# Rotating queries and keys before their norm factor in a two-layer diffusion transformer block

## The chip, the cores and the metric

One core of one Trainium2 chip runs the whole kernel as a single program. The metric is the device time of one execution in microseconds; smaller is better.

## The reference

Two layers work on 1024 image tokens and 256 context tokens of width 1024. Layer 0 mixes a windowed attention (8 query heads, 2 key heads) with a differential attention (4 heads, each with a pair of queries and keys); layer 1 is a gated linear attention, which the change does not touch. In layer 0 each query and key head of 64 numbers is normalised, and for image tokens rotated by its row and column in the token grid:

```python
def rms_norm(x, g):
    xf = x.astype(jnp.float32)
    y = xf * lax.rsqrt(jnp.mean(xf * xf, axis=-1, keepdims=True) + EPS)
    return (y * g.astype(jnp.float32)).astype(x.dtype)

def rope_1d(x, pos):
    ...
    return jnp.concatenate([x1 * cos - x2 * sin, x2 * cos + x1 * sin], axis=-1)

def project(h):
    ...
    qa = rms_norm(qa.reshape(Bn, T, A_HEADS, HEAD_DIM), a_qn)
    ka = rms_norm(ka.reshape(Bn, T, A_KV_HEADS, HEAD_DIM), a_kn)
    ...
qa_x = rope_axial(qa_x, rows, cols)
ka_x = rope_axial(ka_x, rows, cols)
```

The norm factor is one number per token and head, the gain one per place in the head.

## The kernel before

Layer 0's projections and attention are cut into six units, each with its share of the heads: units 0 and 1 belong to the windowed attention (`famA`, 4 query heads and 1 key head), units 2 to 5 to the differential attention (2 and 2). Unit 0 is projected first, beside the loading and the modulation of the inputs. Then, for u = 1 to 6, `layer0_heads` weaves the attention of unit u - 1 with the projection of unit u (for u = 6 with the gates). The windowed attention thus runs beside the projections of units 1 and 2, and the differential one beside those of 3 to 5. The order of each engine's instructions is set when the kernel is built, from the program order, priorities and a model of the times; on the chip every engine works its queue in that order.

A unit has ten token tiles of 128: eight of image tokens, and tiles 8 and 9 of context tokens, which are not rotated. For each, `l0_proj` multiplies (L399) into a PSUM tile `proj` of 384 columns (query heads, key heads, values), and `l0_qkv` (L749) turns it into queries and keys. `l0_qkv` in order:

- In units 0 to 2, where `proj` has four or two banks, it reads PSUM directly (`raw = ps`). In units 3 to 5, with one bank, ACT first copies the tile to SBUF (L163, a `qs` tile).
- ACT squares it into a `qs` tile (L766), DVE sums per head (L768) and scales and adds the epsilon (L769), and POOL raises to the power -0.5 (L223).
- The values are split into a high and a low part (L163, L774).
- DVE multiplies by the norm factor (L776).
- For image tokens the product is multiplied by the cosine table (L784, two instructions, on DVE in units 0 to 2, on POOL in 3 to 5) and, with the halves of each head exchanged, by the sine table (L787, four instructions on POOL), and both are added (L789, on DVE or POOL likewise). Context tokens are multiplied by the gain instead (L793, DVE).
- The result is split into `hb` (L163 and L412, or L807 and L811 on POOL), which TensorE transposes (L817, L821).

The `qs` tiles come from a ring of three (`QS = 3`), which the output gates (L694, L696) use as well in units 0 to 3. `rope_tables` (L500) multiplies the cosine and sine tables by the gains for queries and keys; it runs once for units 0 and 1 and once for units 2 to 5, and its products (L509) are on POOL. Raw weights of the beginning, the modulation weights (L268) and the first two units' projection weights (L584), are staged in a ring of `AW = 17` tiles `aw` of 128x512; SP issues all these loads in order. In the windowed attention POOL also scales the probabilities (L897) and forms the low parts of their transposes (L913).

Of the kernel before, what the change touches and what calls it, by code (L numbers as in the profile page):

```python
# [15 lines left out]
ALU = mybir.AluOpType  # L16
# [3 lines left out]
P = 128  # L20
# [19 lines left out]
AW = 17  # L40
# [93 lines left out]
class K:  # L134
# [307 lines left out]
    def layer0_heads(self, es, esw):  # L442
# [4 lines left out]
        self.pp = self.pool(es, "l0p")  # L447
        with ExitStack() as es1:
            ap = self.ap = self.pool(es1, "l0a")
            self.psum(T="017", O="2", proj="3456")  # L450
            self.condition(ap)
            self.xn = {}
            self.l0_x(4)
            self.staged = 0
            self.hspare = self.st(self.lp, [P, 2, NT * P], "k", F32R, bufs=2).rearrange("p a c -> p (a c)")[
                :, 0:2048].rearrange("p (t a k c) -> p t a k c", t=2, a=2, k=4)
            st = self.l0_state(0)
            drain(self.l0_proj(0, st, True))
# [41 lines left out]
    def rope_tables(self, fam):  # L500

        nc = self.nc
        self.tabs = []
        for j in range(2):
            raw = self.st(self.ap, [P, 512], "sc", bufs=2).rearrange("p (t d) -> p t d", t=NX)
            nc.sync.dma_start(raw, self.a["rope"][:, j])
            t = self.st(self.pp, [P, NX, 2, 64], f"tab{j}")
            for q in range(2):
                nc.gpsimd.tensor_tensor(t[:, :, q, :], raw,  # L509
                                        self.gain[:, 2 * q + j, :].unsqueeze(1).to_broadcast([P, NX, 64]),  # L510
                                        op=ALU.mult)
# [237 lines left out]
    def l0_qkv(self, famA, i, ps, st):  # L749
# [13 lines left out]
        else:  # L763
            raw = ps
        sq = qs()
        nc.scalar.activation(sq[:, 0:nh, :].rearrange("p a d -> p (a d)"), raw[:, 0:w], AF.Square)  # L766
        ss = self.st(pp, [P, 8], "qss", bufs=2)
        nc.vector.tensor_reduce(ss[:, 0:nh], sq[:, 0:nh, :], axis=AX.X, op=ALU.add)  # L768
        nc.vector.tensor_scalar(ss[:, 0:nh], ss[:, 0:nh], 1.0 / 64, EPS, op0=ALU.mult, op1=ALU.add)  # L769
# [5 lines left out]
        xn = qs()  # L775
        (nc.vector if raw is ps else self.by("xn")).tensor_tensor(xn[:, 0:nh, :], raw[:, 0:w].rearrange("p (h d) -> p h d", d=64),  # L776
                                r[:, 0:nh].unsqueeze(2).to_broadcast([P, nh, 64]), op=ALU.mult)
        rq = qs()
        groups = [(0, nq, 0), (nq, nk, 1)]
        if i < NX:  # L780
            m = qs()
            for h0, n, q in groups:
                cosv = self.tabs[0][:, i, q, :].unsqueeze(1).to_broadcast([P, n, 64])
                self.by("cos").tensor_tensor(rq[:, h0:h0 + n, :], xn[:, h0:h0 + n, :], cosv, op=ALU.mult)  # L784
                for s in range(2):
                    sv = self.tabs[1][:, i, q, 32 * s:32 * s + 32].unsqueeze(1).to_broadcast([P, n, 32])
                    nc.gpsimd.tensor_tensor(m[:, h0:h0 + n, 32 * s:32 * s + 32],  # L787
                                            xn[:, h0:h0 + n, 32 - 32 * s:64 - 32 * s], sv, op=ALU.mult)
            self.by("rot").tensor_tensor(rq[:, 0:nh, :], rq[:, 0:nh, :], m[:, 0:nh, :], op=ALU.add)  # L789
        else:  # L790
            for h0, n, q in groups:
                gv = self.gain[:, 2 * q, :].unsqueeze(1).to_broadcast([P, n, 64])
                nc.vector.tensor_tensor(rq[:, h0:h0 + n, :], xn[:, h0:h0 + n, :], gv, op=ALU.mult)  # L793
        hb = self.st(pp, [P, 6, P], "hb", F32R, bufs=1)
        flat = hb.rearrange("p a d -> p (a d)")
        if famA:

            self.split(hb[:, 0:4, 0:64], hb[:, 0:4, 64:128], rq[:, 0:4, :], ("hb", "hblo"))
            kk = rq[:, 4:5, :].to_broadcast([P, 2, 64])
            self.split(hb[:, 4, :].rearrange("p (a d) -> p a d", a=2), hb[:, 5, :].rearrange("p (a d) -> p a d", a=2), kk, ("hb", "hblo"))  # L800
            nqb = 4
        else:
# [917 lines left out]
```

## Time and profile before

| | us |
|---|---|
| median of 3 runs | 1592.39 |
| lowest, highest | 1588.01, 1595.9 |
| the profiled execution | 1597.08 |
| its span | 1595.3 |

| engine | busy us | share of the span |
|---|---|---|
| TensorE, matmul | 1482.9 | 93% |
| TensorE, weight load | 1302.5 | 82% |
| DVE | 1017.0 | 64% |
| ACT | 792.4 | 50% |
| POOL | 579.6 | 36% |

A line such as L787 is line 787 of the kernel. Names before the arrow are what an instruction writes, those behind it what it reads. "PE" is TensorE's matmul, "PEld" its weight load, "SPq" the queue of SyncE that issues DMAs. The idle time before an instruction is put down to whoever released it last.

### The profile page before, as it was taken

Reading aid. Unit: us, or ns where it says so; the run is one execution under the profiler, and the core shown is the slowest. Engines: PE = TensorE matmul, PEld = TensorE weight load, DVE = VectorE, ACT = ScalarE, POOL = GpSimd, SP = SyncE. Lnnn points to the kernel's source line nnn. Section 1 sums busy time; section 2 is a strip of 40 time slices with the busy share of each in tenths; the row PEclk is TensorE's granted clock in tenths of the full one; section 3 lists DMA queues with packets and bytes.
Section 4 is the critical chain, followed back from the end, with each engine's and each line's share of the span. In section 5 each row is a group of like instructions: output and inputs, shape, how many; then the busy total and the mean of one; then the engine's idle time right before and its main releaser. Section 6 shows DMA issues by size and latency. Waiting matters only on the chain.

```text
span 1595.3 us, 26832 instructions
## 1 busy us (share of the span) xinstructions
PE 1482.9 (93%) x9460; PEld 1302.5 (82%) x9460; DVE 1017.0 (64%) x2488; ACT 792.4 (50%) x2153; POOL 579.6 (36%) x857
## 2 busy tenths in 40 slices
PE   6897998999899999999999899989989999997998
PEld 4897977888798877688898777878878998896897
DVE  3787678768667666577765767638854536237565
ACT  3665667776756655466645634345642413224111
POOL 1756777988745554247100000001111212112111
PEclk9898999999999999999999999999999999999999
DMA  9732314322231565623323368655673635425542
GB/s 343 301 145 91 120 67 126 126 70 97 83 115 68 175 230 185 199 83 116 104 80 129 123 198 295 249 187 188 231 242 108 237 132 194 166 94 182 168 149 106
DMA packets 108399, 251.30 MB, mean 158 GB/s; under 512 B 10372, under 2 KB 58500, under 8 KB 94440
## 3 DMA queue, kind: packets, MB, share of 16 engines
q1 hardware_dynamic: 108264, 249.58, 46.1%
q8 instruction: 75, 1.23, 0.3%
q14 instruction: 60, 0.49, 0.1%
HBM read 196.78 MB, written 52.76 MB: 156 GB/s over the span
## 4 chain that ended last, share of the span: by engine, by line
PE 65%; DVE 8%; DMA 7%; ACT 4%; issue 3%; POOL 2%; SPq 0%; ACTq 0%; DVEq 0%; POOLq 0%
PE proj L399 40%; PE SX L1021 4%; PE T L1034 2%; PE AD L242 2%; PE S L399 1%; PE O L942 1%; DMA wraw<-in_w_out 1%; DMA wraw<-in_w_head 1%; PE T L931 1%; PE O L1048 1%; PE O L1046 1%; PE O L1047 1%; PE T L1462 1%; ACT p L993 1%; DMA h<-g_d 1%
## 5 line engine op out<-in xcount | busy, mean ns | idle before, releaser
L399 PE MATMUL proj<-w,h 128*128 128x384 f32 (+2 forms) x2544 | 555.2, 359 | 9.1 <-DVE qs L696 3.8
L399 PEld LDWEIGHTS proj<-w,h 128*128 128x128 f32 x2544 | 437.1, 192 | 49.8 <-DVE qs L696 5.4
L399 PE MATMUL proj<-h,w 128*128 128x256 f32 x1800 | 268.3, 291 | 14.0 <-DVE w L412 2.9
L399 PEld LDWEIGHTS proj<-h,w 128*128 128x128 f32 x1800 | 241.3, 194 | 27.4 <-DVE w L412 4.5
L993 ACT ACTIVATE p<-SX,bnm 128x512 f32<-128x512 f32 (+1 forms) x208 | 124.3, 610 | 52.2 <-DVE bnm L986 38.0
L1444 POOL TENSOR_SCALAR Ts<-U,alpha 128x256 f32<-128x256 f32 x64 | 36.9, 577 | 244.4 <-DVE U L1440 244.4
L913 POOL TENSOR_TENSOR wt<-praw,wt 128x512 fp32r<-128x512 f32 (+1 forms) x96 | 114.8, 1209 | 25.5 <-ACT wt L912 20.6
L1021 PE MATMUL SX<-k,q 128*128 128x512 f32 (+1 forms) x416 | 109.0, 371 | 3.4 <-ACT p L993 3.3
L981 DVE TENSOR_REDUCE bnm<-SX 128x1 f32<-128x512 f32 x128 | 86.2, 685 | 39.9 <-PE SX L1021 39.2
L223 POOL TENSOR_TENSOR qr<-qss,mhalf 128x4 f32<-128x4 f32 (+1 forms) x60 | 65.6, 1094 | 67.5 <-DVE qss L769 62.7
L1021 PEld LDWEIGHTS SX<-k,q 128*128 128x128 f32 x416 | 69.0, 190 | 19.8 <-ACT p L993 7.1
L1440 DVE SCALAR_TENSOR_TENSOR U<-U,alpha,S 128x256 f32<-128x256 f32 x64 | 30.6, 478 | 81.4 <-PE S L399 65.1
L787 POOL TENSOR_TENSOR qs<-qs,tab 128x64 f32<-128x64 f32 (+1 forms) x192 | 73.0, 406 | 11.2 <-DVE qs L776 3.3
L223 POOL TENSOR_TENSOR brr<-brs,mhalf 128x2 f32<-128x2 f32 x20 | 16.6, 831 | 164.3 <-DVE brs L1067 145.2
L414 ACT CAST wt<-T 128x512 fp32r<-128x512 f32 (+1 forms) x104 | 50.8, 511 | 43.9 <-PE T L1034 43.6
L415 DVE TENSOR_TENSOR wt<-T,wt 128x512 fp32r<-128x512 f32 (+1 forms) x104 | 59.1, 580 | 13.6 <-ACT wt L414 13.2
L911 ACT COPY praw<-T 128x512 f32<-128x512 f32 (+1 forms) x96 | 49.6, 542 | 34.8 <-PE T L931 34.2
L414 ACT CAST kmt<-T 128x128 fp32r<-128x128 f32 x72 | 18.7, 266 | 95.0 <-PE S L399 48.2
L897 POOL TENSOR_SCALAR p<-p,arz 128x640 f32<-128x640 f32 (+2 forms) x80 | 59.7, 759 | 15.9 <-DVE arz L895 10.4
L223 POOL TENSOR_TENSOR nr<-nms,mhalf 128x1 f32<-128x1 f32 x20 | 11.7, 586 | 146.4 <-DVE nms L339 146.4
L399 PE MATMUL proj<-w,ohl 128*128 128x512 f32 x240 | 62.0, 402 | 2.6 <-DVE ohl L741 1.7
L414 ACT CAST w<-wraw 128x768 fp32r<-128x768 f32 (+2 forms) x48 | 33.7, 727 | 59.9 <-DMA wraw<-in_w_head 37.1
(310 smaller groups left out, 3395.4 us busy)
## 6 DMA issues: line engine op xcount, KB each, us to landing
h<-hT_d SPq DMA_DIRECT2D x50, 1024.0 KB, 5.0
h<-h_d SPq DMA_DIRECT2D x38, 1024.0 KB, 5.0
aw<-in_adaln_w SPq DMA_DIRECT2D x32, 384.0 KB, 3.8
h_d<-h SPq DMA_DIRECT2D x10, 1024.0 KB, 7.3
wraw<-in_w_head SPq DMA_DIRECT2D x24, 384.0 KB, 4.0
xin<-in_x SPq DMA_DIRECT2D x16, 512.0 KB, 5.5
hT_d<-h SPq DMA_DIRECT2D x8, 1024.0 KB, 5.5
g_d<-qs SPq DMA_DIRECT2D x40, 128.0 KB, 1.7
```

The source lines that it names most:

```text
L223: self.nc.gpsimd.tensor_tensor(out, x, self.mhalf[: x.shape[0], : x.shape[1]], op=ALU.pow)
L399: nc.tensor.matmul(ps, lhsT=x, rhs=y, start=(k == 0 and m == 0), stop=(k == n - 1 and m == 2))
L414: self.nc.scalar.copy(hi, src)
L415: self.nc.vector.tensor_tensor(lo, src, f(hi), op=ALU.subtract)
L787: nc.gpsimd.tensor_tensor(m[:, h0:h0 + n, 32 * s:32 * s + 32], xn[:, h0:h0 + n, 32 - 32 * s:64 - 32 * s], sv, op=ALU.mult)
L897: (nc.vector if hh < PN else nc.gpsimd).tensor_scalar(pv[:, hh], pv[:, hh], rz[:, hh:hh + 1], 0.0, op0=ALU.mult, op1=ALU.add)
L911: (nc.vector.tensor_copy if mode == 2 else nc.scalar.copy)(raw, src)
L913: (nc.vector if mode == 4 else nc.gpsimd).tensor_tensor(lo, raw, f(hi), op=ALU.subtract)
L981: nc.vector.tensor_reduce(nmx[:, s, c:c + 1], B, axis=AX.X, op=ALU.max, negate=True)
L993: nc.scalar.activation(pe[s][:, col:col + w], B, AF.Exp, bias=nm, accum_out=Z[:, s, c:c + 1])
L1021: nc.tensor.matmul(out, lhsT=q[:, 2 * x + s, :], rhs=kk[:, s, ks], start=(x == 0), stop=(x == 1))
L1444: nc.gpsimd.tensor_scalar(t, u, self.alpha[:, 4 * d + h, n:n + 1], 0.0, op0=ALU.mult, op1=ALU.add)
```

## The change

Queries and keys of image tokens are multiplied by the tables first, straight from the projection (PSUM in units 0 to 2, the SBUF copy in 3 to 5), on DVE in units 0 to 2 and on POOL in 3 to 5: one product with the cosine table, one with the sine table in which the halves of each head are read in exchanged order through a negative step. They are added, and the product with the norm factor comes last (L776's, always DVE, now in place). For this the tables are laid out for all five or four heads instead of one for queries and one for keys; `rope_tables` makes them head by head, for units 0 and 1 the query heads on DVE, otherwise on POOL. Context tokens are multiplied by the gain from the projection, on DVE or POOL likewise, and then by the norm factor. The squares go to two tiles of their own with a 65th column that holds the epsilon, scaled by 1/8 before the square, so that the sum of 65 is what the power takes, and L769 goes. In units 0 and 1 the key's split, which was made twice to fill both halves, is made once together with the queries, and POOL copies the block with its halves exchanged. `AW` falls from 17 to 12.

```diff
@@ -37,7 +37,7 @@
 KEEP = 1
 HLP = (4,)
 XNP = 1
-AW = 17
+AW = 12
 XB = 4
 XNB = 4
 W1A = 1
@@ -445,6 +445,9 @@
         self.hlast = None
         self.lp = self.pool(es, "l0b")
         self.pp = self.pool(es, "l0p")
+        self.qsq = [self.st(self.pp, [P, 5, 65], f"qsq{j}") for j in range(2)]
+        for t in self.qsq:
+            self.nc.gpsimd.memset(t[:, :, 64:65], EPS)
         with ExitStack() as es1:
             ap = self.ap = self.pool(es1, "l0a")
             self.psum(T="017", O="2", proj="3456")
@@ -501,14 +504,16 @@
 
         nc = self.nc
         self.tabs = []
+        nq, nk = ((2, 2), (4, 1))[fam == 0]
         for j in range(2):
             raw = self.st(self.ap, [P, 512], "sc", bufs=2).rearrange("p (t d) -> p t d", t=NX)
             nc.sync.dma_start(raw, self.a["rope"][:, j])
-            t = self.st(self.pp, [P, NX, 2, 64], f"tab{j}")
-            for q in range(2):
-                nc.gpsimd.tensor_tensor(t[:, :, q, :], raw,
-                                        self.gain[:, 2 * q + j, :].unsqueeze(1).to_broadcast([P, NX, 64]),
-                                        op=ALU.mult)
+            t = self.st(self.pp, [P, NX, 5, 64], f"tab{j}")
+            for q, h0, n in ((0, 0, nq), (1, nq, nk)):
+                e = nc.vector if fam == 0 and q == 0 else nc.gpsimd
+                for h in range(h0, h0 + n):
+                    e.tensor_tensor(t[:, :, h, :], raw,
+                                    self.gain[:, 2 * q + j, :].unsqueeze(1).to_broadcast([P, NX, 64]), op=ALU.mult)
             self.tabs.append(t)
 
     def l0_consts(self):
@@ -762,43 +767,38 @@
                 self.copy("raw", raw[:, 0:UC], ps[:, 0:UC])
         else:
             raw = ps
-        sq = qs()
-        nc.scalar.activation(sq[:, 0:nh, :].rearrange("p a d -> p (a d)"), raw[:, 0:w], AF.Square)
+        on = nc.vector if raw is ps else nc.gpsimd
+        sq = self.qsq[i % 2][:, 0:nh, :]
+        nc.scalar.activation(sq[:, :, 0:64], raw[:, 0:w].rearrange("p (h d) -> p h d", d=64), AF.Square, scale=0.125)
+        rh = raw[:, 0:w].rearrange("p (h d) -> p h d", d=64)
+        rq = qs()[:, 0:nh, :]
+        if i < NX:
+            m = qs()[:, 0:nh, :]
+            on.tensor_tensor(rq, rh, self.tabs[0][:, i, 0:nh, :], op=ALU.mult)
+            on.tensor_tensor(m.rearrange("p h (s d) -> p h s d", s=2),
+                             rh.rearrange("p h (s d) -> p h s d", s=2)[:, :, ::-1, :],
+                             self.tabs[1][:, i, 0:nh, :].rearrange("p h (s d) -> p h s d", s=2), op=ALU.mult)
+            self.by("rot").tensor_tensor(rq, rq, m, op=ALU.add)
+        else:
+            for h0, n, q in ((0, nq, 0), (nq, nk, 1)):
+                on.tensor_tensor(rq[:, h0:h0 + n, :], rh[:, h0:h0 + n, :],
+                                 self.gain[:, 2 * q, :].unsqueeze(1).to_broadcast([P, n, 64]), op=ALU.mult)
         ss = self.st(pp, [P, 8], "qss", bufs=2)
-        nc.vector.tensor_reduce(ss[:, 0:nh], sq[:, 0:nh, :], axis=AX.X, op=ALU.add)
-        nc.vector.tensor_scalar(ss[:, 0:nh], ss[:, 0:nh], 1.0 / 64, EPS, op0=ALU.mult, op1=ALU.add)
+        nc.vector.tensor_reduce(ss[:, 0:nh], sq, axis=AX.X, op=ALU.add)
         r = self.st(pp, [P, 8], "qr", bufs=2)
         self.rsqrt(r[:, 0:nh], ss[:, 0:nh])
         v = st["v"][i] = self.st(lp, [P, 256], "v", F32R, bufs=20)
         self.copy("vhi", v[:, 0:vd], raw[:, w:UC])
         (nc.vector if raw is ps else self.by("vlo")).tensor_tensor(v[:, vd:2 * vd], raw[:, w:UC], f(v[:, 0:vd]), op=ALU.subtract)
-        xn = qs()
-        (nc.vector if raw is ps else self.by("xn")).tensor_tensor(xn[:, 0:nh, :], raw[:, 0:w].rearrange("p (h d) -> p h d", d=64),
-                                r[:, 0:nh].unsqueeze(2).to_broadcast([P, nh, 64]), op=ALU.mult)
-        rq = qs()
-        groups = [(0, nq, 0), (nq, nk, 1)]
-        if i < NX:
-            m = qs()
-            for h0, n, q in groups:
-                cosv = self.tabs[0][:, i, q, :].unsqueeze(1).to_broadcast([P, n, 64])
-                self.by("cos").tensor_tensor(rq[:, h0:h0 + n, :], xn[:, h0:h0 + n, :], cosv, op=ALU.mult)
-                for s in range(2):
-                    sv = self.tabs[1][:, i, q, 32 * s:32 * s + 32].unsqueeze(1).to_broadcast([P, n, 32])
-                    nc.gpsimd.tensor_tensor(m[:, h0:h0 + n, 32 * s:32 * s + 32],
-                                            xn[:, h0:h0 + n, 32 - 32 * s:64 - 32 * s], sv, op=ALU.mult)
-            self.by("rot").tensor_tensor(rq[:, 0:nh, :], rq[:, 0:nh, :], m[:, 0:nh, :], op=ALU.add)
-        else:
-            for h0, n, q in groups:
-                gv = self.gain[:, 2 * q, :].unsqueeze(1).to_broadcast([P, n, 64])
-                nc.vector.tensor_tensor(rq[:, h0:h0 + n, :], xn[:, h0:h0 + n, :], gv, op=ALU.mult)
+        self.by("xn").tensor_tensor(rq, rq, r[:, 0:nh].unsqueeze(2).to_broadcast([P, nh, 64]), op=ALU.mult)
         hb = self.st(pp, [P, 6, P], "hb", F32R, bufs=1)
         flat = hb.rearrange("p a d -> p (a d)")
         if famA:
 
-            self.split(hb[:, 0:4, 0:64], hb[:, 0:4, 64:128], rq[:, 0:4, :], ("hb", "hblo"))
-            kk = rq[:, 4:5, :].to_broadcast([P, 2, 64])
-            self.split(hb[:, 4, :].rearrange("p (a d) -> p a d", a=2), hb[:, 5, :].rearrange("p (a d) -> p a d", a=2), kk, ("hb", "hblo"))
+            self.split(hb[:, 0:5, 0:64], hb[:, 0:5, 64:128], rq, ("hb", "hblo"))
             nqb = 4
+            nc.gpsimd.tensor_copy(hb[:, 5, :].rearrange("p (a d) -> p a d", a=2),
+                                  f(hb[:, 4, :]).rearrange("p (a d) -> p a d", a=2)[:, ::-1, :])
         else:
 
             qh, ql = [hb[:, 2 * x:2 * x + 2, :].rearrange("p b (a d) -> p b a d", a=2) for x in range(2)]
```

## Rows read from the trace of the kernel before

**Rows 1.** the page: busy time of each engine; the chain that ended last, by engine

```profile
PE 1482.9 (93%) x9460; PEld 1302.5 (82%) x9460; DVE 1017.0 (64%) x2488; ACT 792.4 (50%) x2153; POOL 579.6 (36%) x857
PE 65%; DVE 8%; DMA 7%; ACT 4%; issue 3%; POOL 2%; SPq 0%; ACTq 0%; DVEq 0%; POOLq 0%
```

**Rows 2.** single lines L776, L784, L789: ns min/median/max, first and last start

```profile
L776 DVE TENSOR_TENSOR qs<-proj,qr x30: 409/481/493, 54.3 to 399.2; 128x320 f32<-128x320 f32 x20, 128x256 f32<-128x256 f32 x10
L776 DVE TENSOR_TENSOR qs<-qs,qr x30: 413/425/1516, 423.4 to 759.1; 128x256 f32<-128x256 f32 x30
  POOL qr L223: 20.9, 28
...
L784 DVE TENSOR_TENSOR qs<-qs,tab x48: 213/481/1379, 66.9 to 399.9; 128x256 f32<-128x256 f32 x16, 128x64 f32<-128x64 f32 x16, 128x128 f32<-128x128 f32 x16
...
L789 DVE TENSOR_TENSOR qs<-qs,qs x24: 406/493/1572, 77.3 to 401.9; 128x320 f32<-128x320 f32 x16, 128x256 f32<-128x256 f32 x8
```

**Rows 3.** five stretches: busy us of each engine, clock, DMA

```profile
core 0: us, PE busy (x) PEld busy (x) DVE busy (x) ACT busy (x) POOL busy (x), PEclk, DMA share, GB/s
63.00:118.00 55.00, 49.80 (x317) 46.48 (x318) 42.54 (x101) 34.44 (x88) 29.65 (x40) 0.97 0.45 176
118.00:270.00 152.00, 135.08 (x869) 121.99 (x867) 112.86 (x327) 96.40 (x291) 107.01 (x135) 0.93 0.31 102
270.00:410.00 140.00, 129.34 (x858) 116.20 (x856) 104.51 (x279) 100.61 (x297) 121.01 (x154) 0.98 0.29 94
410.00:775.00 365.00, 348.83 (x2237) 298.69 (x2237) 239.97 (x623) 219.77 (x644) 189.25 (x322) 0.98 0.41 139
300.00:325.00 25.00, 20.43 (x133) 17.31 (x131) 17.90 (x44) 17.06 (x51) 24.14 (x30) 0.93 0.29 104
```

**Rows 4.** pieces of the chain that ended last: start us, us, what

```profile
188.67 1.28 POOL qs L787 x4
...
219.02 1.72 DVE qs L784 x2
...
390.85 0.94 DVE qs L789
...
499.87 1.81 POOL qs L787 x2
```

**Rows 5.** groups by line and shape, 0 to 800 us: busy us, mean ns

```profile
L787 POOL TENSOR_TENSOR qs<-qs,tab 128x64 f32<-128x64 f32 x128 | 47.1, 392 | 1.9 <-DVE arz L895 1.5
...
L784 POOL TENSOR_TENSOR qs<-qs,tab 128x128 f32<-128x128 f32 x48 | 22.5, 472 | 17.3 <-DVE qs L776 13.9 <-DVE brz L1002 1.2 <-DVE bzs L1000 1.1
...
L789 POOL TENSOR_TENSOR qs<-qs,qs 128x256 f32<-128x256 f32 x24 | 18.6, 776 | 1.6
...
L787 POOL TENSOR_TENSOR qs<-qs,tab 128x128 f32<-128x128 f32 x32 | 16.9, 549 | 9.3 <-DVE qs L776 3.3 <-DVE anms L881 1.9 <-DVE adl L883 1.3
...
L789 DVE TENSOR_TENSOR qs<-qs,qs 128x320 f32<-128x320 f32 x16 | 11.3, 706 | 4.7 <-POOL qs L787 4.3
...
L784 DVE TENSOR_TENSOR qs<-qs,tab 128x256 f32<-128x256 f32 x16 | 10.7, 668 | 0.2
...
L787 POOL TENSOR_TENSOR qs<-qs,tab 128x32 f32<-128x32 f32 x32 | 9.7, 321 | 0.0
```

**Rows 6.** what writes or reads the rotation tables, and who waited

```profile
L787 POOL TENSOR_TENSOR qs<-qs,tab x192: 243/324/1662, 75.5 to 762.2; 128x64 f32<-128x64 f32 x128, 128x128 f32<-128x128 f32 x32, 128x32 f32<-128x32 f32 x32
...
L509 POOL TENSOR_TENSOR tab<-sc,gn x8: 1273/1286/1442, 40.2 to 306.1; 128x512 f32<-128x512 f32 x8
...
  ACT qs L163: 5.2, 4
```

**Rows 7.** groups by line and shape, 0 to 120 us

```profile
L412 DVE TENSOR_TENSOR w<-aw,w 128x512 fp32r<-128x512 f32 x16 | 12.2, 776 | 11.4 <-ACT w L163 11.2
```

**Rows 8.** the order of time: SP's queue, TensorE's loads (start us, us)

```profile
24.10 4.86 SPq L268 DMA_DIRECT2D aw<-in_ada  x8
...
24.75 0.16 PEld L271 LDWEIGHTS O<-aw,s 128*32 128x32 f32 x8
```

## The prediction

> **What bounds the kernel now.** I read the page first, then the stretches, then single lines. Over the whole run TensorE is the busiest engine, 93% by matmuls and 82% by weight loads [rows 1], and two thirds of the chain that ended last is its own work; DVE, ACT and POOL together hold 14% of that chain [rows 1]. But the change touches only `l0_qkv`, `rope_tables` and one buffer count, and `l0_qkv` lives in the first half: its norm products (L776) run from 54.3 to 399.2 us reading PSUM (units 0 to 2, 30 tiles) and from 423.4 to 759.1 reading an SBUF copy (units 3 to 5, 30 tiles) [rows 2]. So I cut the time there. In the four stretches of [rows 3] TensorE is idle 55 - 49.8 = 5.2, 152 - 135.1 = 16.9, 140 - 129.3 = 10.7 and 365 - 348.8 = 16.2 us. The middle two are units 1 and 2, with the windowed attention beside the projection: there POOL is busy 107 of 152 and 121 of 140 us, DVE 113 and 105, and the granted clock is 0.93 and 0.98. TensorE is the fullest engine there too, but it waits for chains that hop between DVE, POOL and ACT; that, and the clock lost after such waits, is what a change of this kind can win. All idle TensorE time from 63 to 410 us is 32.8 us, which caps it.
>
> The tile's own chain is visible in the waits of its lines. The normalising product (L776) comes behind POOL's power (L223), for which DVE stood idle 20.9 us in 28 places [rows 2]; behind it come cosine (L784), sine (L787) and sum (L789), and only then the splits and the transposes. In the chain that ended last, ten pieces of at least 0.85 us between 188 and 391 us are these three lines alone: 1.28 + 1.72 + 0.85 + 1.36 + 1.43 + 1.46 + 1.05 + 1.13 + 1.58 + 0.94 = 12.8 us, and one more of 1.81 us lies at 499.87 ([rows 4] has the first, the largest and the last of the ten, and that one). No piece of the chain before 180 us can be read.
>
> **The change part by part.** *Sine on POOL, units 0 and 1.* Removed per rotated tile: two products of 128x128 at 549 ns and two of 128x32 at 321 ns, 1.74 us [rows 5]. Added per tile: a POOL copy of the doubled key block, for which no row exists; bounds are 0.24 us (the shortest product on POOL, L787's minimum [rows 6]) and 0.55 (L787's 128x128 products [rows 5]); I take 0.47, the mean of L784 on POOL, which has the same element count [rows 5]. Eight rotated tiles of ten: 8 x 1.74 - 10 x 0.47 = 9.2 us less POOL per unit. *Unit 2*: 8 x 4 x 0.392 = 12.5 us less [rows 5].
>
> *DVE, units 0 to 2.* Before: the norm product from PSUM (0.48 [rows 2]), cosine for the queries (0.668 [rows 5]) and for the key (0.21 at least, the minimum in [rows 2]): 1.36 us. After: two products straight from PSUM, 0.48 each, and the norm product from SBUF, with the shape and the sources of L789, 0.706 [rows 5]: 1.67 us. The sum stays. One small scalar operation and, in units 0 and 1, the second pair of split instructions go. I count DVE as even. What matters is the place: all of it but the norm product now runs beside POOL's power instead of behind it, so the chain is shorter by sine or cosine plus the sum. PSUM is also let go without waiting for the power. The reversed read in the sine product is in no row; it has the element count of its neighbour, so 0.48, or at worst the two halves apart, 0.2 us more.
>
> Here the trace says something on contention. Products that read PSUM took 409 to 493 ns and never more; those with both sources in SBUF took up to 1379, 1516 and 1572 ns [rows 2]. The Trainium skill, SBUF — State Buffer, "Who interferes with whom", says that a DVE instruction with two SBUF inputs contends with a POOL instruction that reads SBUF, and one with at most one SBUF input does not; the trace agrees by these maxima. By that rule the change frees the cosines but exposes the norm product, which now stands alone behind the power; by it alone each of the 24 rotated tiles of units 0 to 2 would have its 0.48 turned into as much as 1.57, 26 us of DVE at the most, and by the mean of 0.706 it is 5.4, less what the freed cosines give back.
>
> *Units 3 to 5.* POOL drops two cosines (0.472), four sines (0.392) and keeps the sum: 3.29 us; it gets three full products of 0.776, 2.33 us [rows 5]. Context tiles move two gain products from DVE to POOL, 2 x 0.47. Per unit 8 x 0.96 - 2 x 0.94 = 5.8 us less. These products start from the raw copy and no longer stand behind the power. Also, the ring of three `qs` buffers carries raw, product and sine instead of five tiles: ACT's raw copy waited 5.2 us in 4 places for POOL's sine because of that ring [rows 6], and the projection behind it has one bank there, so that wait reaches TensorE.
>
> *Tables.* Five heads instead of two. At the start eight query products go to DVE and two key products stay on POOL (four before, 1.29 us each [rows 6]). DVE's nearest row, 128x512 with two SBUF sources, took 776 ns in the mean [rows 7]: 8 x 0.776 = 6.2 us. DVE can hide it: the first user is the first cosine, at 66.9 us [rows 2], and the inputs are there at 40.2, when POOL's first table product runs [rows 6]. Without that cover it is 6.2 us in front of the splits that feed TensorE. I take 2, bounds 0 and 6.2. In unit 2 POOL builds eight instead of four: 4 x 1.29 = 5.1 us more, around 300 us, where POOL is busy 24.1 of 25 us [rows 3], so hardly any cover; but the same stretch loses 12.5 us of sines. I take 2, bounds 0 and 5.1.
>
> *The smaller ring of staged weights, 17 to 12.* With 12 the thirteenth tile takes the first one's place. In the eight issues spaced 0.61 us from 24.10 on, the sixth (at 27.2) needs the buffer of the first of the five before, which TensorE had read from 24.75 on [rows 8]; a slack of about 2 us, and the four before that wait only for weight splits of the earlier columns. I take 0. If that slack is gone, SP's queue stops there, and x, gain and rope loads behind it come later by as much.
>
> The rest is next to nothing: POOL writes the epsilon column once into each of two tiles, and the sum of squares runs over 65 instead of 64 numbers per head.
>
> **The sum.** Pieces of the three lines on the chain from 180 to 410: 12.8 us, bounds 0 and 12.8; something else is next late (attention's own softmax chain), so I take two thirds, 8.5. From 63 to 180, where the chain is not to be seen, the same density would be 12.8 x 117 / 230 = 6.5; TensorE is idle little there, so 2.5. Units 3 to 5: 0 to 4.5 (the piece of 1.81 and half of the raw waits), 2. Clock: 0.93 over 152 us is 10.6 us of clock withheld, given back only where a wait disappears wholly: 2, bounds 0 and 5. Less 2 + 2 for tables. Net 8.5 + 2.5 + 2 + 2 - 4 = 11.0 us. The profiled execution took 1597.08 us (span 1595.3), 4.7 above the median of 1592.39; 1597.1 - 11.0 = 1586.1 there, and on the median 1581.4.
>
> **The rivals.** *No change that can be told.* Attention's softmax sets the pace of units 1 and 2 and the rotation merely came last by a hair; TensorE's stream is what counts. For it: TensorE is 93% busy and 86% of the chain holds none of DVE, ACT, POOL [rows 1]. Against it: 12.8 us of pieces. Time: gain 3 minus tables 3, 1592. The Trainium skill, Perfetto Trace Analysis, "Identifying the Most-Contended Engine", would side with it: optimise the engine with the highest occupancy, which is not one of those relieved here; the trace bears that out for the whole span, less in the stretches of units 1 and 2.
>
> *POOL is the bound of units 1 and 2.* In unit 2 it is busy 121 of 140 us, 86% [rows 3]. Then its lost work counts in full: 9.2 for unit 1, 12.5 - 5.1 = 7.4 for unit 2, with 2.5 before, 2 after, 2 from the clock: 23, 1569. Against it: in unit 1 POOL is only 70% busy.
>
> *Slower: the tables come ahead of the splits.* DVE's eight table products stand early in the program; if they sit in its queue ahead of the first hidden-state splits, TensorE waits for all 6.2 us at about 40 us, POOL's 5.1 us at 300 stall the first rotated tile of unit 2, and one drop of the clock of half the size seen in unit 1 follows, 5.3. Less a gain of 5 that remains: 6.2 + 5.1 + 5.3 - 5 = 11.6 slower, 1604. It decides from the point where DVE has under 6.2 us free between 40.2 and 66.9 us; from 63 on it is free 12.5 of 55 [rows 3].
>
> **How the numbers follow.** Forecast 0.42, POOL bound 0.17, no change 0.27, slower 0.14. I predict 1581 us. The range takes in every gain at its upper bound with no costs, 12.8 + 6.5 + 4.5 + 5 = 28.8, to 1564, and reaches 1600 upward, most of the way to the slower case. A measurement of this kernel tells about 0.5% (8 us) from no change. Faster by more: all of the POOL case, nearly all of the forecast, little else: 0.57. Within: 0.29. Slower by more: 0.14.
>
> **What would show it.** Right: after the power only the norm product and the splits follow, and the sum and the two rotation products vanish from the chain; ACT's raw copy no longer waits for POOL; POOL falls by some 9 us in unit 1 and 7 in unit 2; TensorE's idle time between 118 and 410 falls from 27.6 to below 20 us. Wrong: TensorE idle there is unchanged with other releasers (attention), or a new idle stretch stands at 40 to 66 us or at 300 with the tables before it, or the norm product takes well over 0.7 us.

## The result and the profile after

| | before | after |
|---|---|---|
| median, us | 1592.93 (4 runs) | 1569.99 (4 runs) |
| lowest, highest | 1588.01, 1595.9 | 1563.11, 1576.49 |
| the profiled execution | 1597.08 | 1573.26 |
| its span | 1595.3 | 1571.5 |

The ratio of after to before is 0.985, with an interval from 0.9818 to 0.9882: 23 us faster, where 11 were forecast (1581, range 1564 to 1600). The direction and the range were right; the size that was forecast is half of what came. One of the rivals, POOL as the bound, had named 1569.

The page of after, busy time of each engine (us, share of the span, instructions) and the chain that ended last by engine; it answers to [rows 1]:

```profile
PE 1477.3 (94%) x9460; PEld 1298.9 (83%) x9460; DVE 986.9 (63%) x2394; ACT 791.4 (50%) x2143; POOL 540.3 (34%) x701
PE 68%; DMA 13%; DVE 8%; ACT 5%; issue 3%; POOL 3%; SPq 0%; ACTq 0%; DVEq 0%; POOLq 0%
```

POOL lost 579.6 - 540.3 = 39 us of work, DVE 1017.0 - 986.9 = 30 us. The same stretches as in [rows 3], of after:

```profile
core 0: us, PE busy (x) PEld busy (x) DVE busy (x) ACT busy (x) POOL busy (x), PEclk, DMA share, GB/s
63.00:118.00 55.00, 53.47 (x373) 52.11 (x371) 40.98 (x102) 34.79 (x84) 24.29 (x27) 1.00 0.44 170
118.00:270.00 152.00, 145.32 (x977) 134.06 (x978) 110.87 (x322) 108.38 (x325) 110.45 (x121) 0.98 0.34 112
270.00:410.00 140.00, 129.72 (x829) 115.52 (x827) 91.66 (x251) 99.94 (x292) 116.34 (x123) 0.94 0.28 91
410.00:775.00 365.00, 351.83 (x2315) 303.79 (x2314) 242.44 (x608) 221.41 (x653) 155.69 (x222) 0.99 0.42 142
```

The stretches are cut at the same times, so they hold different work. The number of matmuls tells it: from 63 to 270 us TensorE did 373 + 977 = 1350 where it had done 317 + 869 = 1186, and from 270 to 410 fewer than before, 829 for 858. The gain was made before 270 us. The matmuls can also serve as a clock: how many had started by 63, 180 and 410 us before, and when after had started as many.

```profile
0.00:63.00 63.00, 46.40 (x458) 37.33 (x458) 31.11 (x82) 31.48 (x69) 25.93 (x32) 0.95 0.93 344
0.00:180.00 180.00, 149.71 (x1120) 133.50 (x1121) 115.81 (x323) 101.18 (x268) 93.87 (x125) 0.93 0.57 209
0.00:410.00 410.00, 360.62 (x2497) 322.00 (x2497) 291.02 (x786) 262.93 (x744) 283.60 (x360) 0.95 0.42 146
```

and after:

```profile
0.00:66.30 66.30, 48.38 (x458) 37.86 (x459) 37.16 (x96) 34.65 (x75) 28.58 (x38) 0.92 0.95 353
0.00:168.10 168.10, 145.56 (x1119) 130.87 (x1120) 108.71 (x299) 101.14 (x260) 82.47 (x98) 0.96 0.59 218
0.00:391.00 391.00, 354.59 (x2497) 318.44 (x2497) 267.30 (x734) 263.41 (x735) 262.90 (x287) 0.96 0.43 152
```

After is 3.3 us behind at the first point, then 11.9 and 19.0 ahead. So the stretch from 63 to 180 us gave some 15 us, that from 180 to 410 some 7. The two kernels' matmuls are not in quite the same order, so these are estimates. A fixed mark in the work shows it too. The squares of the first and the last tile of unit 0 and of the last tile of unit 1, ACT in order of time (start us, us), before:

```profile
48.83 0.43 ACT L766 ACTIVATE qs<-proj 128x320 f32<-128x320 f32 x1
...
125.18 0.44 ACT L766 ACTIVATE qs<-proj 128x320 f32<-128x320 f32 x1 [0.97 <-DVE arz L895]
...
245.17 0.44 ACT L766 ACTIVATE qs<-proj 128x320 f32<-128x320 f32 x1 [0.57 <-issue]
```

and after:

```profile
52.21 0.44 ACT L772 ACTIVATE qsq<-proj 128x320 f32<-128x320 f32 x1
...
111.34 0.43 ACT L772 ACTIVATE qsq<-proj 128x320 f32<-128x320 f32 x1
...
221.47 0.44 ACT L772 ACTIVATE qsq<-proj 128x320 f32<-128x320 f32 x1 [0.55 <-PE proj L399]
```

The first comes 3.4 us later, the second 13.8 us earlier, the third 23.7 us earlier. So unit 0 gave 17 us from its first to its last square, unit 1 another 10. The last product of the windowed attention (L942) started at 434.2 us before and starts at 415.3 now, 18.9 us earlier: unit 2 gave 5 us back. Before and after:

```profile
L942 PE MATMUL O<-wt,v x168: 388/396/505, 146.8 to 434.2; 128*128 128x512 f32 x168
L942 PE MATMUL O<-wt,v x168: 388/396/794, 137.5 to 415.3; 128*128 128x512 f32 x168
```

From there to the end the lead goes from 18.9 to 23.8 us.

Where unit 0's loss had stood can be read around its end. Before, the stretches 120 to 130 and 130 to 140 us:

```profile
120.00:130.00 10.00, 5.64 (x33) 4.74 (x33) 7.52 (x37) 4.34 (x17) 6.16 (x15) 0.78 0.32 96
130.00:140.00 10.00, 7.31 (x28) 6.96 (x27) 4.89 (x18) 4.44 (x16) 5.20 (x9) 0.54 0.15 36
```

and after, from 110 us on, since unit 0 ends earlier there:

```profile
110.00:120.00 10.00, 7.30 (x56) 7.06 (x54) 8.65 (x31) 4.12 (x12) 1.96 (x4) 1.00 0.10 27
120.00:130.00 10.00, 10.00 (x61) 9.78 (x62) 8.01 (x35) 6.71 (x26) 6.50 (x12) 0.83 0.38 133
130.00:140.00 10.00, 10.00 (x75) 9.59 (x74) 4.97 (x18) 7.51 (x21) 7.96 (x8) 1.00 0.26 106
```

Before, the last tiles of unit 0 were still on their way through DVE and POOL when attention began; TensorE stood idle 7 of 20 us, the granted clock fell to 0.54, which is mostly the lower of its two levels (1.2 of 2.4 GHz), and 61 matmuls were done. After has the same break at 110 to 120 us, but a shorter one: 2.7 us of idle time, then a clock of 0.83 in the next 10 us. From 100 to 160 us, which holds both breaks, TensorE was busy 50.9 us before and 57.3 after.

The single lines of after, ns min/median/max, first and last start; L777 and L778 are the two rotation products, L781 their sum, L793 the norm product, L800 POOL's copy of the key block. They answer to [rows 2]:

```profile
L777 DVE TENSOR_TENSOR qs<-proj,tab x24: 406/481/492, 65.1 to 373.8; 128x320 f32<-128x320 f32 x16, 128x256 f32<-128x256 f32 x8
...
L778 DVE TENSOR_TENSOR qs<-proj,tab x24: 406/478/492, 65.5 to 374.2; 128x320 f32<-128x320 f32 x16, 128x256 f32<-128x256 f32 x8
...
L781 DVE TENSOR_TENSOR qs<-qs,qs x24: 407/482/1755, 66.2 to 375.1; 128x320 f32<-128x320 f32 x16, 128x256 f32<-128x256 f32 x8
...
L793 DVE TENSOR_TENSOR qs<-qs,qr x60: 409/450/1590, 55.8 to 734.1; 128x256 f32<-128x256 f32 x40, 128x320 f32<-128x320 f32 x20
  POOL qs L781: 9.4, 5
  POOL qr L223: 8.1, 9
...
L800 POOL CAST hb<-hb x20: 284/291/672, 59.2 to 251.2; 128x128 fp32r<-128x128 f32 x20
```

The read in exchanged order (L778, 478 ns) costs what the plain one costs (L777, 481). DVE's idle time before the norm product that ended with POOL's power went from 20.9 us to 8.1 [rows 2]; 9.4 us that ended with POOL's sum (L781, units 3 to 5) are new.

### The profile page after: what moved, and what is told of

Read it like the earlier page. It is cut to its first block, busy times and chain, and to the rows that moved or that the text cites. A ratio compares the mean times of both kernels' runs of the same rounds, so it can differ in the third digit from the quotient of the medians.

```text
span 1571.5 us, 26566 instructions
## 1 busy us (share of the span) xinstructions
PE 1477.3 (94%) x9460; PEld 1298.9 (83%) x9460; DVE 986.9 (63%) x2394; ACT 791.4 (50%) x2143; POOL 540.3 (34%) x701
## 4 chain that ended last, share of the span: by engine, by line
PE 68%; DMA 13%; DVE 8%; ACT 5%; issue 3%; POOL 3%; SPq 0%; ACTq 0%; DVEq 0%; POOLq 0%
PE proj L399 43%; PE SX L1021 4%; DMA wraw<-in_w_head 3%; PE T L1034 2%; PE O L942 2%; PE AD L242 2%; PE T L931 2%; PE S L399 1%; DMA D<-D_d 1%; PE O L1048 1%; PE O L1046 1%; DMA wraw<-in_w_out 1%; PE O L1047 1%; PE T L817 1%; PE T L376 1%
## 5 line engine op out<-in xcount | busy, mean ns | idle before, releaser
L399 PEld LDWEIGHTS proj<-w,h 128*128 128x128 f32 x2544 | 434.2, 191 | 52.8 <-issue 9.3
L414 ACT CAST wt<-T 128x512 fp32r<-128x512 f32 (+1 forms) x104 | 50.9, 511 | 44.4 <-PE T L1034 44.0
L911 ACT COPY praw<-T 128x512 f32<-128x512 f32 (+1 forms) x96 | 50.2, 542 | 35.8 <-PE T L931 32.6
L897 POOL TENSOR_SCALAR p<-p,arz 128x640 f32<-128x640 f32 (+2 forms) x80 | 61.8, 786 | 16.6 <-ACT praw L911 6.7
L1034 PE MATMUL T<-ident,p 128*128 128x128 f32 x336 | 54.1, 281 | 5.6 <-DVE brz L1002 2.9
```

Source lines behind the costliest of these rows:

```text
L399: nc.tensor.matmul(ps, lhsT=x, rhs=y, start=(k == 0 and m == 0), stop=(k == n - 1 and m == 2))
L414: self.nc.scalar.copy(hi, src)
L897: (nc.vector if hh < PN else nc.gpsimd).tensor_scalar(pv[:, hh], pv[:, hh], rz[:, hh:hh + 1], 0.0, op0=ALU.mult, op1=ALU.add)
L911: (nc.vector.tensor_copy if mode == 2 else nc.scalar.copy)(raw, src)
L1034: nc.tensor.transpose(tp[:, b, :], wv[:, (b0 + b) * P:(b0 + b + 1) * P], self.ident)
```

## The experiments

All are compared with the kernel before on the same chip in the same runs. Times are medians; the intervals are of the ratio to the kernel before.

| kernel | median us | ratio, interval |
|---|---|---|
| after | 1570.0 | 0.9818 to 0.9882 |
| e9: after, values' split moved | 1569.5 | 0.982 to 0.9889 |
| e1: new order in units 0 to 2 only | 1571.8 | 0.9826 to 0.991 |
| e17: after, POOL load in unit 2 | 1574.4 | 0.9852 to 0.9905 |
| e18: after, inputs' product on DVE | 1575.1 | 0.9869 to 0.9918 |
| e19: after, low halves on DVE | 1578.6 | 0.9882 to 0.9945 |
| e3: after, norm product first | 1580.0 | 0.9879 to 0.9941 |
| e7: after, tables of unit 2 on DVE | 1581.1 | 0.9884 to 0.9957 |
| e12: after, tables of two heads | 1581.9 | 0.9915 to 0.9961 |
| e4: before, 12 staged tiles | 1584.2 | 0.9927 to 0.9973 |
| e6: after, first tables all on POOL | 1584.5 | 0.9934 to 0.9975 |
| e16: after, POOL load in unit 0 | 1585.2 | 0.9926 to 0.997 |
| e10: before, 15 staged tiles | 1587.2 | 0.9954 to 0.9989 |
| e11: after, POOL load in units 0 to 2 | 1589.4 | 0.995 to 1.0005 |
| e2: new order in units 3 to 5 only | 1590.4 | 0.9964 to 1.0003 |
| e14: before, 12 tiles, values' split moved | 1590.6 | 0.9961 to 0.9992 |
| e5: before, 12 tiles, ring of 5 | 1590.7 | 0.9966 to 1.0008 |
| e15: before, sines on DVE | 1592.8 | 0.9977 to 1.001 |
| e8: before, values' split moved | 1599.3 | 1.0015 to 1.0045 |

**Which units.** The new order in one half of the units only; the other half keeps the old instructions (tables, epsilon column, split and ring as in after).

```diff
-        rq = qs()[:, 0:nh, :]
+        if raw is ps:          # e1; e2 has "raw is not ps"
+            rq = qs()[:, 0:nh, :]
...
+        if raw is not ps:      # the old norm, cosine, sine, sum, behind the power
```

> The changed kernel, but units 3 to 5 keep the norm product first and the cosine and sine in six instructions on POOL, as before. Theory A (rotation behind the power is what cost, and most of it in units 0 to 2): 1573 to 1579, that is 14 to 20 of the 23 us stay. Theory B (the raw copy and its ring in units 3 to 5 carry half): 1580 to 1586. Theory C (the new order of all queues is luck and any edit loses it): anywhere from 1570 to 1595, with unit marks before 400 us changed as well.

> The changed kernel, but units 0 to 2 keep the norm product first, cosine on DVE in two and sine on POOL in four instructions. Theory A: 1586 to 1592, only the 6 us or so of units 3 to 5 are won, less the larger tables. Theory B: 1580 to 1584. Theory C: no relation to e1; the gains of e1 and e2 do not add up to 23 us.

Measured 1571.8 and 1590.4. Units 0 to 2 carry the gain, all but some 2 us; units 3 to 5 alone give 2.5 us with an interval that reaches to no change. Theory A named the range of e2, and e1 lies 1.3 us below its range; B is out. The two gains add up to 23.5 us, so C has no support here. Both kernels hold the parts that all units share: larger tables, epsilon column, single key split, 12 staged tiles. That the gains add up all the same, and that e2 as a whole gives 2.5 us, says that these parts together are worth next to nothing in e2.

**The place or the work.** e3 puts the norm product back ahead of the two whole-tile products, in all units, on the same engines.

```diff
-            on.tensor_tensor(rq, rh, self.tabs[0][:, i, 0:nh, :], op=ALU.mult)
+            self.by("xn").tensor_tensor(xn, rh, r[:, 0:nh].unsqueeze(2)..., op=ALU.mult)
+            on.tensor_tensor(rq, xn, self.tabs[0][:, i, 0:nh, :], op=ALU.mult)
```

> The changed kernel with the norm product put back ahead of the two rotation products, which stay two whole-tile instructions on the same engines. It has the changed kernel's POOL and DVE work, but the rotation stands behind the power again. Theory A (place): most of the gain is lost, 1582 to 1592. Theory P (POOL's work was the bound of units 1 and 2, the rival of the prediction): nearly all stays, 1568 to 1575.

e11 leaves the place and gives POOL products of the old sines' shapes as idle work (with 11 staged tiles); e16 does so in unit 0 alone, e17 in unit 2 alone.

```diff
+            if raw is ps:      # e16: self.cls == 0; e17: raw is ps and not famA
+                for h0, n in ((0, nq), (nq, nk)):
+                    for s in range(2):
+                        nc.gpsimd.tensor_tensor(dm[:, 0:n, 32 * s:32 * s + 32], self.tabs[0][...], sv, op=ALU.mult)
```

> The changed kernel, with POOL given back the four sine products per rotated tile of units 0 to 2, in the old shapes, reading the tables and writing a scratch tile that nobody reads (11 staged weight tiles instead of 12, for room). The rotation stays ahead of the norm product. If POOL's load was the bound of units 1 and 2: 1583 to 1592, the unit marks up to 410 us lose 10 us or more. If the place counts: 1569 to 1576.

> The changed kernel with the idle sine products on POOL in unit 0 alone (14 us of POOL). If unit 0 is where POOL binds, about half of the 19 us that all three units lost: 1577 to 1583, and the last square of unit 0 comes some 9 us later than in the changed kernel. If not: 1568 to 1574.

> The changed kernel with the idle sine products on POOL in unit 2 alone (12.5 us of POOL), where POOL was busiest before (86%). If POOL binds there: 1576 to 1583. If the end of attention sets unit 2's end by another engine: 1568 to 1574.

e3 was between the theories, 1580.0: with the whole-tile products kept, the place is worth 10 of the 23 us (the intervals of e3 and after just touch). For the other part e3 is to be read against e2, 1590.4, which has the old instructions in units 0 to 2 at the same place behind the power. The pages of e2 and e3:

```profile
PE 1485.6 (94%) x9460; PEld 1300.6 (82%) x9460; DVE 999.1 (63%) x2394; ACT 789.5 (50%) x2143; POOL 576.0 (36%) x797
PE 1473.6 (94%) x9460; PEld 1289.5 (82%) x9460; DVE 998.4 (64%) x2394; ACT 789.2 (50%) x2143; POOL 541.4 (34%) x701
```

Two products on DVE instead of two cosines on DVE and four sines on POOL: POOL loses 35 us of work, DVE's work stays the same, and the kernel is 10 us faster, although e3 lacks the new order of units 3 to 5 that e2 has. The step from DVE to POOL and back behind the power goes with it, so whether the 10 us are POOL's load or that step is open.

e11 took back 19.4 us, e16 alone 15.2, e17 4.4, the last within the noise of after. Their expectations took this for the price of the old sines; it isn't. The idle products need only the tables, and the build put them where no sine had stood. In e16 all 32 run between 40.6 and 60.0 us, 22 of them in one go; before, the first sine starts at 75.5 us [rows 6]. In e11 those of units 0 and 1 run between 40.8 and 93 us. e16, in order of time:

```profile
48.75 8.61 POOL L787 TENSOR_TENSOR dm<-tab,tab 128x32 f32<-128x32 f32 x22
...
60.17 1.27 POOL L387 TENSOR_TENSOR k<-h,k 128x512 fp32r<-128x512 f32 x1
...
61.50 3.57 PE L399 MATMUL proj<-w,k 128*128 128x384 f32 x10 [5.48 <-POOL k L387]
...
121.08 0.43 ACT L772 ACTIVATE qsq<-proj 128x320 f32<-128x320 f32 x1
```

TensorE waits 5.5 us there for a low half of the hidden states (L387), which stands behind the idle products on POOL; the last square of unit 0 comes at 121.08 us, against 111.34 in after. The stretch from 40 to 80 us, e16 and after, 31.6 and 37.7 us of TensorE:

```profile
40.00:80.00 40.00, 31.63 (x200) 26.19 (x195) 24.46 (x62) 20.84 (x51) 32.01 (x54) 0.80 0.64 239
40.00:80.00 40.00, 37.74 (x264) 33.91 (x265) 30.51 (x77) 26.25 (x66) 26.84 (x27) 0.88 0.78 293
```

The smaller ring of 11 isn't the cause: e17 has it too, and its last square of unit 0 is at 111.43. So work on POOL ahead of the hidden states' low halves costs much; what POOL's old sines cost at their own place in units 0 and 1 these runs do not show.

**POOL alone?** e15 is the kernel before with the sines of units 0 to 2 on DVE and nothing else. e18 and e19 take ten and eight products from POOL in unit 0 of after and give them to DVE (POOL's busy time falls by 13.6 and 9.5 us).

```diff
-                    nc.gpsimd.tensor_tensor(m[:, h0:h0 + n, 32 * s:32 * s + 32],
+                    (nc.vector if raw is ps else nc.gpsimd).tensor_tensor(m[:, h0:h0 + n, 32 * s:32 * s + 32],   # e15
-XNP = 1
+XNP = 0          # e18
-HLP = (4,)
+HLP = ()         # e19
```

> The kernel before with one edit: the four sine products of units 0 to 2 are on DVE instead of POOL; norm product first, 17 staged tiles, old tables. POOL loses 1.7 us per rotated tile, DVE gains four instructions of 0.2 to 0.5 us. If POOL is the bound of units 0 to 2: 1580 to 1587. If the place of the rotation counts: 1590 to 1598. If DVE is as near to its limit: 1595 to 1605.

> The changed kernel with the product that normalises the inputs (L343, ten of 1.25 us on POOL in unit 0) on DVE. If POOL still binds unit 0 after the change: 1558 to 1566. If DVE, 77% busy between 40 and 120 us, is as near to its limit: 1570 to 1580.

> The changed kernel with the low halves of the hidden states (L387, eight of 1.3 us on POOL in unit 0) on DVE, where the other halves are made already. If POOL still binds unit 0: 1560 to 1567. If DVE does: 1570 to 1580.

e15 changed nothing that can be told (0.9977 to 1.001), and POOL's lost time is there to see; its stretch from 40 to 120 us has 40.0 us of POOL where before 51.0 stood, and 64.0 of DVE where 61.8 stood (before, then e15). From 40 to 410 us POOL lost 35 us and DVE gained 14.

```profile
40.00:120.00 80.00, 73.38 (x462) 68.83 (x463) 61.77 (x140) 50.65 (x128) 50.98 (x60) 0.94 0.59 222
40.00:120.00 80.00, 72.83 (x459) 70.00 (x460) 64.02 (x163) 51.28 (x127) 40.03 (x35) 0.91 0.58 217
```

e18 and e19 are 5 and 9 us slower than after, e18 within the noise; neither is faster. So freeing POOL at DVE's cost does not pay: what one engine sheds, the other must not get. The change took work from both, 39 us and 30 us, by making one instruction of several.

**The ring of `qs` tiles and the staged tiles.**

```diff
-AW = 17
+AW = 12          # e4; e10 has 15; e5 and e14 have 12
-QS = 3
+QS = 5           # e5
```

> The kernel before with 12 instead of 17 staged weight tiles and nothing else. By the prediction no change, 1588 to 1596. If the smaller ring holds up the loads of the beginning, slower by the 3 to 5 us by which the first square came later in the changed kernel (52.2 against 48.8 us): 1595 to 1598. If the ring's size shifts the order for the better: below 1585.

> The kernel before with 12 staged weight tiles and a ring of 5 instead of 3 qs tiles. If the ring was what held back the tile chain in unit 0 and in units 3 to 5 (the change puts two tiles less into it per token tile), 1574 to 1580, and the first 125 us are shorter than with 12 tiles alone. If not, as with 12 tiles alone, 1581 to 1588.

> The kernel before with 15 staged weight tiles. If a smaller ring itself is better, between 17 and 12: 1584 to 1592. If 12 happens to give a good order: 1592 to 1600, or no relation.

Twelve tiles alone make the kernel before 8.5 us faster, 15 tiles 5.5 us. With the wider ring of `qs` tiles the kernel is 6.5 us slower than e4, outside both of its expected ranges; that ring wasn't what held it back. The beginning of e4 is later, its first square at 53.4 us, 4.5 later than before, and the modulation loads that came in one run at 24.10 [rows 8] are split in SP's queue, in order of time:

```profile
24.28 1.63 SPq L268 DMA_DIRECT2D aw<-in_ada  x3
26.19 0.97 SPq L557 DMA_DIRECT2D xin<-in_x  x2
...
33.26 4.74 SPq L268 DMA_DIRECT2D aw<-in_ada  x5
```

The same break is in after. What is lost by it at the beginning comes back later: the last product of the windowed attention (L942) is at 421.1 us, 13 us earlier than in the kernel before.

```profile
L942 PE MATMUL O<-wt,v x168: 388/396/629, 145.5 to 421.1; 128*128 128x512 f32 x168
```

Why the kernel runs faster behind a later start isn't shown.

**What an order is worth.** e8, e9 and e14 move two lines, the split of the values, ahead of the sum of the squares, in before, in after, and in before with 12 tiles. No instruction changes.

> The kernel before with nothing but two lines moved: the split of the values is written ahead of the sum of the squares. The same instructions, other places in the queues. If the order that the build happens to find is worth little, 1588 to 1597. If it is worth as much as the 8.5 us that 12 staged tiles gave, anywhere from 1582 to 1603, and then single differences under some 8 us say nothing of a cause.

> The changed kernel with the same two lines moved. Little worth: 1567 to 1574. Much: 1560 to 1580. If the gain of the change is more than luck of order, it stays over 12 us below its partner with the same move.

> The kernel before with 12 staged tiles and the two lines of the values' split moved. If the 8.5 us that 12 tiles gave belong to the ring, 1582 to 1591 (8 below the 1599 of the same move alone). If they were an order found by luck: 1592 to 1602.

Moved: before 5 to 6 us slower (1.0015 to 1.0045), before with 12 tiles 6 us slower than e4, after unchanged (1569.5). So the order that the build happens to find is worth some 6 us, and single differences of that size say nothing. The change keeps its gain under this move, 29.8 us between e8 and e9; the 12 tiles keep theirs, 8.8 us between e8 and e14.

**The tables.** e6 makes all tables of units 0 and 1 on POOL, e7 the query tables of units 2 to 5 on DVE, e12 tables of two heads for those units, with three rotation products per tile.

```diff
-                e = nc.vector if fam == 0 and q == 0 else nc.gpsimd
+                e = nc.gpsimd                                   # e6
+                e = nc.vector if q == 0 else nc.gpsimd          # e7
-        nq, nk = ((2, 2), (4, 1))[fam == 0]
+        nq, nk = ((1, 1), (4, 1))[fam == 0]                     # e12
```

> The changed kernel with all tables of units 0 and 1 on POOL as well: DVE loses the eight products that it made in one stretch from 35.8 to 44.4 us; POOL makes ten, 13 us. If DVE's stretch held up the beginning: 1564 to 1568, first square before 50 us. If DVE was waiting there for loads anyway: 1568 to 1574. If POOL's 13 us hold up the normalised inputs: 1574 to 1582.

> The changed kernel with the query tables of units 2 to 5 made on DVE, as those of units 0 and 1 are. In the changed kernel POOL made eight tables in one go of 9.9 us at 283 us and TensorE's clock fell there; DVE was about 65% busy in that unit. If that block cost 5 us or more: 1562 to 1567. If DVE then holds up attention's maxima instead: 1568 to 1576.

> The changed kernel with tables of two heads in units 2 to 5 (four POOL products at about 283 us instead of eight, 5.1 us less), at the price of three rotation products per tile instead of two there. If the block of tables costs what it holds POOL, 1560 to 1567, and units 2's end comes 3 to 6 us earlier. If the clock fall there has another cause: 1568 to 1576.

None of the three kept to its expected ranges; all are slower than after. e6: 14.5 us slower, and its last square of unit 0 comes at 116.57 instead of 111.34. The eight products that after makes on DVE hold that engine from 35.8 to 44.4 us, 8.6 us, but TensorE was waiting for a modulation load then, not for DVE. After, in order of time:

```profile
35.77 1.40 DVE L515 TENSOR_TENSOR tab<-sc,gn 128x512 f32<-128x512 f32 x1 [0.53 <-DMA sc<-in_rope]
36.60 3.37 POOL L515 TENSOR_TENSOR tab<-sc,gn 128x512 f32<-128x512 f32 x2
37.16 7.21 DVE L515 TENSOR_TENSOR tab<-sc,gn 128x512 f32<-128x512 f32 x7
...
40.98 3.27 PE L271 MATMUL O<-aw,s 128*32 128x128 f32 x40 [4.59 <-DMA aw<-in_ada]
```

In unit 2 after has POOL making eight tables in one run:

```profile
283.20 9.89 POOL L515 TENSOR_TENSOR tab<-sc,gn 128x512 f32<-128x512 f32 x8
```

and the stretch around it is bad, TensorE 19.5 of 25 us at a clock of 0.73. Before has its four tables at 300 to 307 us, and TensorE 20.4 of 25 us at 0.93 there [rows 3], so the longer block shows mostly in the clock. After:

```profile
275.00:300.00 25.00, 19.45 (x105) 15.97 (x103) 16.68 (x50) 17.43 (x58) 23.92 (x25) 0.73 0.25 83
```

With the block halved the last square of unit 2 comes at 366.5 us (e7) and 362.1 (e12) instead of 373.4. But the windowed attention ends where it did, at 414.6 and 415.1 instead of 415.3; e12:

```profile
L950 PE MATMUL O<-wt,v x168: 388/396/776, 135.2 to 415.1; 128*128 128x512 f32 x168
```

So the block costs nothing at the end of the windowed attention, and both kernels lose their 11 to 12 us behind it. In e7 nothing but the queues' order differs there. In e12 the third product is new as well, and the two can't be told apart. No kernel here was faster than after.

## Why the prediction was right and wrong

The parts that held. The rotation products no longer stand behind the power; TensorE's idle time from 118 to 410 us fell from 27.6 to 6.7 + 10.3 = 17.0 us, below the 20 that were named as the sign. Units 3 to 5 were taken at 2 us; e1 and e2 have 1.8 and 2.5, both within the noise. The reversed read costs nothing. ACT's raw copy waits 2.8 us in one place for POOL instead of 5.2 in four [rows 6]. One sign held in part only: the two products and their sum did not vanish from the chain that ended last. From 180 to 410 us their pieces add up to 4.4 us, where the prediction had read 12.8 for the old lines in pieces of 0.85 us or more; from 410 to 780, where they are on POOL, they still add up to 7.6.

The step that failed is the term for 63 to 180 us: "TensorE is idle little there, so 2.5". By the count of matmuls that stretch gave some 15 us, and unit 0's last square came 13.8 us earlier. The stretch from 180 to 410, the main term with 8.5 and 2 more for the clock, gave some 7. So the forecast put the gain into units 1 and 2, and most of it came in unit 0 and at its end. Two things were misread. The chain of waits did not reach back there, and its place was taken by TensorE's idle time in a stretch that ended at 118 us; but about half of what unit 0's late tiles cost stood behind that, between 120 and 140 us, as idle time and a low clock, and was counted to unit 1: the lead by matmuls goes from 3.3 us behind at 63 us to some 5 ahead at 118 and some 12 at 140. And the 317 matmuls from 63 to 118 us were read as a nearly full engine, 49.8 of 55 us; with 53.5 us it did 373.

The second term of wrong size is the ring, taken at 0. The slack of 2 us was worked out for issues in the old order; the build put the loads into another order, and the first square came later by 3.4 us in after and 4.5 us in e4. All the same e4 is 8.5 us faster as a whole. That does not simply add to the rest: e2 has the 12 tiles too and is 2.5 us faster than before. What 17 tiles would do to the changed kernel was not tried.

Tables: taken at 2 + 2. At the beginning DVE took 8.6 us for its eight products, 1.08 each where 0.776 was reckoned, some as long as 1.75 beside POOL's two of 1.7; it hid all of it, and the choice of DVE saved 14.5 us against POOL (e6). In unit 2 the 5.1 us that were added show as a fall of the clock and cost nothing by the end of the windowed attention.

The rivals. POOL as the bound had the number, 1569, by luck: it put 16.6 of its 23 us into units 1 and 2, where 5 to 7 were won by either count, and e15 shows that freeing POOL at DVE's cost gives nothing. What is shown is that work put on POOL ahead of the normalised inputs and the hidden states' low halves in unit 0 costs 14 to 15 us (e16, e6), that moving load to DVE does not pay (e15, e18, e19), that the two products in place of six are worth 10 us at the old place (e2, e3), and that the new place is worth 10 more (e3, after). The rival of no change leaned on TensorE's 93%. The page of the Trainium skill named there, Perfetto Trace Analysis, "Identifying the Most-Contended Engine", judges TensorE by MFU (its share of peak work) and by its weight loads rather than by its busy share in matmuls. The weight loads were at 82% in the whole span [rows 1], which left room. The slower rival's block of tables came on DVE at 35.8 to 44.4 us, and its 8.6 us were not lost: the chain that ended last holds a load of unit 0's weights there, from 39.0 to 44.2 us.

On contention, products from PSUM stayed within 406 to 492 ns (L777, L778), and those with two SBUF sources reached 1755 and 1590 (L781, L793), as the Trainium skill, SBUF — State Buffer, "Who interferes with whom", would have it. The norm product's mean for five heads in after is 664 ns; 706 was reckoned.

Open: why a smaller ring helps the kernel before, what POOL's old sines cost at their own place in units 0 and 1, and how far the 23 us hold parts of a lucky order; the two lines moved cost before 6 us and after nothing, so each of the two halves of 10 us stands not far above what an order alone can do.

## What to carry to other kernels

Where stages follow each other, time a stage by a mark in its work (the first and last instruction of a kind), not by an engine's idle time between fixed times: what a late stage costs shows in the next one, as idle time and a low clock. Work that two helper engines share is worth removing, not moving; one whole-tile instruction for several small ones took load from both and was worth 10 us here, and taking the products off the path another 10. Before idle work is read as the price of real work, see in the trace where it ran. Where a build sets the order of the queues, move two lines that change nothing first, to learn what an order alone is worth; here 6 us.

## What the runs showed of the hardware that was not expected

A read with a negative step over blocks of 32 numbers costs a DVE product nothing (478 against 481 ns from PSUM) and a POOL product next to nothing at the median (740 against 738 ns; single ones took up to 2052). POOL's copy of 128x128 took 291 ns at the median, where 470 was reckoned from a product of the same size. DVE's 128x512 products of two SBUF sources took 676 ns at least and 1038 at the median beside POOL's own, which took up to 1712 instead of 1278. After, L778 with the exchanged read and L777 without it on POOL, and the table products:

```profile
L777 POOL TENSOR_TENSOR qs<-qs,tab x24: 728/738/748, 399.4 to 726.7; 128x256 f32<-128x256 f32 x24
L778 POOL TENSOR_TENSOR qs<-qs,tab x24: 724/740/2052, 400.1 to 729.2; 128x256 f32<-128x256 f32 x24
L515 POOL TENSOR_TENSOR tab<-sc,gn x10: 1264/1278/1712, 36.6 to 291.8; 128x512 f32<-128x512 f32 x10
L515 DVE TENSOR_TENSOR tab<-sc,gn x8: 676/1038/1750, 35.8 to 43.7; 128x512 f32<-128x512 f32 x8
```
